# A hybrid decoder step on one core: the samples' float32 products of both output halves in one visit per group, raw weight blocks kept until then, sums in rooms of their own

## The chip, the cores and the metric

One core of a Trainium2 chip runs the whole program; the other seven are idle. The metric is device time in microseconds (us) of that core, the median of three runs. PE is the matrix engine, DVE, ACT and POOL are the vector, scalar and general engines, SP issues most of the DMAs and has one queue, taken in order.

## The reference, cut to what matters

One layer of a hybrid decoder. Its tokens are 256 of a prompt and 64 of samples (8 sequences of 8). The part of interest is the last one, a feed-forward block behind a short convolution over time:

```python
def conv_ffn(h, conv_state, w_up, conv_w, conv_b, w_down):
    up = h @ w_up                                   # 2048 -> 2 x 5632
    up, new_conv = causal_depthwise_conv(up, conv_state, conv_w, conv_b)
    g, u = jnp.split(up, 2, axis=-1)
    return (jax.nn.gelu(g, approximate=True) * u) @ w_down, new_conv   # 5632 -> 2048
```

Its result is normed over the 2048 columns and added to the input. Everything is float32 in and out.

## The kernel before, in words

**Numbers.** A matrix product of the prompt is made of float32r matmuls: a weight block is split into a high part (`whi`, a rounded copy by ACT) and a low part (`wlo`, the rest, by DVE), and three matmuls (hi x hi, hi x lo, lo x hi) make one product. A weight block of 128 x 1024 that is treated so is called a slab. Slabs of the up-projection come through three raw rooms (`wraw`); `whi` and `wlo` have three rooms each too, which slabs and the blocks of the down-projection share in turn. So the copy of a slab can begin only when the matmuls of the third slab or block before it are done.

**Groups.** The 5632 inner columns are taken in 11 groups of 512 (`NG` = 11). `ffn_up(g)` makes group g: 24 matmuls of 128 x 320 for each slab, 16 slabs, then convolution, gelu and product on DVE, ACT and POOL. Between the slabs of `ffn_up(g)` stand the steps of the down-projection of the group before it, `down_steps(g - 1, ...)`, a generator that the loop around the slabs advances. Groups 0 to 9 of the down-projection go through `down_steps`; the last goes through `down_plain`.

**One group of the down-projection.** `down_steps` takes the 2048 output columns in two halves (`m`; group 0 takes half 1 first). A half is a product of 512 x 1024 weights, cut into four raw blocks `b11, b12, b21, b22` of 128 x 1024, loaded by SP. The prompt's part is made with seven products in place of eight (Strassen's scheme in Winograd's form): besides the blocks it takes the differences

- `t1 = b12 - b11`, `t3 = b22 - b12`, `t2 = b22 - t1`, `t4 = t2 - b21`,

which POOL makes in quarters of 256 columns (`less`), in the order given. The seven products come in the order 1 (`b11`), 2 (`b21`), 5 (`t1`), 7 (`t3`), 3 (`b22`), 6 (`t2`), 4 (`t4`), one a step, with a slab between one and the next. Each (`product`) has its block split by ACT and DVE (`ready`) and six matmuls of 128 x 512 (`pm`), and its sum is added by DVE to one of seven kept sums (`taken_in`; in group 0 ACT copies it).

**The samples.** The 64 sample tokens take the blocks as they are, in float32. `sample_products` issues four matmuls for two blocks, on the two column halves of the array; one half's samples are eight matmuls (16 in the trace, which shows each as two), into one PSUM tile `pms`. They stand between products 1 and 2 of each half. So in each group the engine goes twice from float32r to float32 and back. One such stretch of float32 matmuls is called a visit here.

**Rooms.** In a half, `t3` is written over `b12`, `t2` over `b11` and `t4` over `b21`, all after the visit; `t1` has a room of its own. The sums of half 0 lie in the room `in_mix` (where the layer's `acc_mix` was), those of half 1 in `in_fp`. Two rooms under the tag `gain` hold first the four blocks of tokens that are turned in group 0 and stored (`to_rows`, `in_turn`, `x1_rows`), and from group 4 on the last norm's gains, loaded behind that group.

The order of the work on each engine is fixed at build time, by a scheduler that keeps each engine's program in order of priority; `tc.high_priority` and `tc.issue_after` steer it.

Of the kernel before, what the change touches and what calls it, by code (L numbers as in the profile page):

```python
# [16 lines left out]
P = 128  # L17
# [16 lines left out]
def hybrid_step(  # L34
# [111 lines left out]
    bg, side, due, made_so_far, last_made = [], [], {}, [0], [None]  # L146
# [178 lines left out]
    def add_square(total, x, begins, adder=pool, place=("sq", 2)):  # L325
        if begins:
            act.activation(total, x, AF.Square)
        else:
            sq = tp.tile([P, NT], F32, tag=place[0], name="sq", bufs=place[1])
            act.activation(sq, x, AF.Square)  # L330
            adder.tensor_tensor(out=total, in0=total, in1=sq, op=ALU.add)

    def squares_of(total):
# [3 lines left out]
        def step(nb):  # L337
# [6 lines left out]
            with first():  # L344
                if nb < KD - 1:
                    held.append(misc("sq_ps")[:, :NT])
                else:
                    one.append(tp.tile([P, NT], F32, tag="sq", name="sq", bufs=2))
# [80 lines left out]
    with ExitStack() as mctx:  # L429
        op = mctx.enter_context(tc.tile_pool(name="op", bufs=1))  # L430
        bT = op.tile([P, 4, NT], F32, name="bT")
# [157 lines left out]
        with tc.tile_pool(name="gp", bufs=1) as gp:  # L589
# [196 lines left out]
            def gate_mix(g, uf, res):  # L786
# [17 lines left out]
                for m in range(2):  # L804
# [8 lines left out]
                    for i, ps in enumerate(both):  # L813
                        j = 2 * m + i
                        s = tp.tile([P, NT], F32, tag="ev", name="s", bufs=2)
# [44 lines left out]
        with tc.tile_pool(name="sd", bufs=1) as sd:  # L860
# [318 lines left out]
            def heads_out(g):  # L1179
# [4 lines left out]
                def z_evac(j, ps):  # L1184
                    while y_made.get(g, -1) < j:
                        advance(bg, bg[0])
                    zs = tp.tile([P, NT], F32, tag="ev", name="zs", bufs=2)
# [119 lines left out]
    with tc.tile_pool(name="fp", bufs=1) as fp:  # L1307
# [148 lines left out]
        sums_of_m, f_s, taken = [None, None], [None, None], []  # L1456

        def room_for_sums(m):

            room = fp.tile([P, 8, 512], F32, name="in_fp") if m else hp.tile([P, 8, 512], F32, tag="acc_mix", name="in_mix")  # L1460
# [24 lines left out]
        def down_steps(ck, parts):  # L1485
# [8 lines left out]
            last_rows = kept_rows[0]  # L1494
            for _ in range(3 if ck == 0 else 1 if ck == NG - 2 else 2):
                yield
            for m in (1, 0) if ck == 0 else (0, 1):
                raw = {}
                if ck == 0:
                    room_for_sums(m)  # L1500

                def load(name):
                    k, n = int(name[1]) - 1, int(name[2]) - 1
                    raw[name] = fp.tile([P, 1024], F32, name=name)
                    with tc.high_priority(offset=100000), tc.issue_after(slab_load[-1]) if ck == 0 else nullcontext():
                        sp.dma_start(raw[name].rearrange("p (k n) -> p k n", n=512), rows_of(ffn_w_down, 4 * ck + 2 * k, 2, 1024 * m + 512 * n, 512))

                def less(to, x, y):
                    with tc.high_priority(offset=100000), tc.issue_after(last_rows):
                        for q in range(0, 1024, 256):  # L1510
                            cs = slice(q, q + 256)
                            pool.tensor_tensor(out=to[:, cs], in0=raw[x][:, cs], in1=raw[y][:, cs], op=ALU.subtract)  # L1512

                def product(i, x, w):
                    hi, lo = ready(raw[w])
                    ps = misc("pm")
                    prompt_products(ps, (parts.hi[x], parts.lo[x]), (hi, lo), True, True)
                    taken_in(sums_of_m[m][i - 1], ps, ck == 0)

                for name in ("b11", "b12", "b22", "b21"):  # L1520
                    load(name)
                product(1, "a11", "b11")
# [325 lines left out]
```

## Time and profile before

| | |
|---|---|
| three runs | 1740.63 us median (1740.51 to 1740.68) |
| the profiled execution | 1738.82 us, span 1737.1 us, granted PE clock 0.998 |
| PE busy | 1722.9 us, 99% of the span |
| PE's weight loads | 1605.9 us, 92% |
| DVE busy | 1363.9 us, 79% |
| ACT busy | 878.5 us, 51% |
| POOL busy | 684.8 us, 39% |
| DMA | 310.60 MB, 179 GB/s in the mean |

The span is the time from the first to the last instruction; the profiled execution lies 1.72 us above its span, and 1.81 us below the median of the runs. A row of the timeline or of a group names line, engine, operation, what is written and what is read, and shapes as partitions x elements; names come without the numbers of their buffers, so `b11` to `b22` are all `b`, and `t1` is `t`. In square brackets stands idle time of the engine before the instruction and what ended it. Groups 0 to 9 of the down-projection run from about 873 us to 1686 us.

### The profile page before, as it was taken

Reading aid. Unit: us, or ns where it says so; the run is one execution under the profiler, and the core shown is the slowest. Engines: PE = TensorE matmul, PEld = TensorE weight load, DVE = VectorE, ACT = ScalarE, POOL = GpSimd, SP = SyncE. Lnnn points to the kernel's source line nnn. Section 1 sums busy time; section 2 is a strip of 40 time slices with the busy share of each in tenths; the row PEclk is TensorE's granted clock in tenths of the full one; section 3 lists DMA queues with packets and bytes.
Section 4 is the critical chain, followed back from the end, with each engine's and each line's share of the span. In section 5 each row is a group of like instructions: output and inputs, shape, how many; then the busy total and the mean of one; then the engine's idle time right before and its main releaser. Section 6 shows DMA issues by size and latency. Waiting matters only on the chain.

```text
span 1737.1 us, 29944 instructions
## 1 busy us (share of the span) xinstructions
PE 1722.9 (99%) x11223; PEld 1605.9 (92%) x11223; DVE 1363.9 (79%) x2137; ACT 878.5 (51%) x1272; POOL 684.8 (39%) x999
## 2 busy tenths in 40 slices
PE   9999999999999999999999999999999999999997
PEld 9999999999999999999988898888888889888884
DVE  6549864657969788788987778888887879798898
ACT  6344545333656565645565444444444444454443
POOL 2432230000423423112355556565655555555552
PEclk9999999999999999999999999999999999999999
DMA  8786664556676777665765544545445454545445
GB/s 265 215 240 184 185 177 148 157 163 191 202 225 197 227 221 220 205 199 164 241 185 156 158 147 148 159 142 178 150 145 171 144 166 150 164 149 160 148 143 161
DMA packets 216018, 310.60 MB, mean 179 GB/s; under 512 B 22080, under 2 KB 118976, under 8 KB 215680
## 3 DMA queue, kind: packets, MB, share of 16 engines
q1 hardware_dynamic: 198624, 279.76, 53.1%
q0 software_dynamic: 6176, 13.87, 2.6%
q10 hardware_dynamic: 11072, 15.05, 2.5%
q8 instruction: 88, 1.44, 0.4%
q14 instruction: 58, 0.48, 0.1%
HBM read 285.00 MB, written 22.32 MB: 177 GB/s over the span
## 4 chain that ended last, share of the span: by engine, by line
PE 96%; DVE 2%; issue 1%; ACT 0%; POOL 0%; DVEq 0%; ACTq 0%; POOLq 0%
PE ps L135 20%; PE ps L137 20%; PE ps L136 20%; PE pm L1475 11%; PE pd L135 4%; PE pd L137 4%; PE pd L136 4%; PE pms L1482 4%; PE y_ps L1088 1%; PE ps_v L135 1%; PE ps_v L136 1%; PE ps_v L137 1%; DVE wlo L125 0%; PE yo_ps L1003 0%; PE up_ps L1020 0%
## 5 line engine op out<-in xcount | busy, mean ns | idle before, releaser
L135 PE MATMUL ps<-h_hi,whi 128*128 128x320 f32 x2428 | 750.2, 309 | 0.0
L137 PE MATMUL ps<-h_hi,wlo 128*128 128x320 f32 x2428 | 749.0, 309 | 0.1
L136 PE MATMUL ps<-h_lo,whi 128*128 128x320 f32 x2428 | 748.6, 308 | 0.0
L125 DVE TENSOR_TENSOR wlo<-wraw,whi 128x1024 fp32r<-128x1024 f32 (+2 forms) x394 | 487.4, 1238 | 146.0 <-ACT whi L124 144.2
L124 ACT CAST whi<-wraw 128x1024 fp32r<-128x1024 f32 (+2 forms) x393 | 405.1, 1031 | 372.9 <-PE ps L136 143.1
L135 PEld LDWEIGHTS ps<-h_hi,whi 128*128 128x128 f32 x2428 | 455.6, 188 | 9.1 <-issue 1.3
L136 PEld LDWEIGHTS ps<-h_lo,whi 128*128 128x128 f32 x2428 | 455.9, 188 | 6.3
L137 PEld LDWEIGHTS ps<-h_hi,wlo 128*128 128x128 f32 x2428 | 455.5, 188 | 0.7 <-DVE wlo L125 0.6
L1491 DVE TENSOR_TENSOR wlo<-b,whi 128x1024 fp32r<-128x1024 f32 x120 | 155.1, 1292 | 74.4 <-ACT whi L1490 74.2
L1490 ACT CAST whi<-b 128x1024 fp32r<-128x1024 f32 x120 | 125.5, 1046 | 161.9 <-PE ps L136 144.1
L1512 POOL TENSOR_TENSOR b<-b,b 128x256 f32<-128x256 f32 x160 | 184.8, 1179 | 0.0
L135 PE MATMUL pd<-ohi,whi 128*128 128x320 f32 x448 | 138.7, 310 | 0.0
L137 PE MATMUL pd<-ohi,wlo 128*128 128x320 f32 x448 | 138.3, 309 | 0.0
L136 PE MATMUL pd<-olo,whi 128*128 128x320 f32 x448 | 138.3, 309 | 0.0
L1358 POOL COPY ptf<-pad 128x2 f32<-128x2 f32 x88 | 39.2, 446 | 187.2 <-DVE pad L1346 186.6
L1512 POOL TENSOR_TENSOR b<-b,t 128x256 f32<-128x256 f32 x80 | 76.8, 969 | 86.0 <-PE pms L1482 86.0
L1512 POOL TENSOR_TENSOR t<-b,b 128x256 f32<-128x256 f32 x80 | 89.5, 1148 | 14.7 <-DMA b<-in_ffn_w_down 14.7
L135 PEld LDWEIGHTS pd<-ohi,whi 128*128 128x128 f32 x448 | 84.1, 188 | 0.6
L136 PEld LDWEIGHTS pd<-olo,whi 128*128 128x128 f32 x448 | 84.1, 188 | 0.3
L137 PEld LDWEIGHTS pd<-ohi,wlo 128*128 128x128 f32 x448 | 84.1, 188 | 0.0
L248 DVE TENSOR_TENSOR acc_mix<-acc_mix,pd 128x320 f32<-128x320 f32 (+1 forms) x113 | 53.7, 478 | 27.8 <-PE pd L137 27.5
L1482 PE MATMUL pms<-b,a_s 128*64 128x512 f32 x320 | 73.1, 598 | 0.0
(415 smaller groups left out, 2490.4 us busy)
## 6 DMA issues: line engine op xcount, KB each, us to landing
wraw<-in_ffn_w_up SPq DMA_DIRECT2D x176, 512.0 KB, 4.5
wraw<-in_w_in SPq DMA_DIRECT2D x132, 512.0 KB, 3.9
b<-in_ffn_w_down SPq DMA_DIRECT2D x80, 512.0 KB, 4.5
wraw<-in_w_out SPq DMA_DIRECT2D x64, 512.0 KB, 3.5
st<-in_state_ssm SPq DMA_DIRECT2D x40, 256.0 KB, 4.4
out_ssm_state_sample<-st ACTq DMA_DIRECT2D x30, 256.0 KB, 2.4
cs<-dacs_d SPq DMA_DIRECT2D x16, 320.0 KB, 5.3
wraw<-in_w_in SPq DMA_DIRECT2D x12, 384.0 KB, 4.3
```

Of the source, the lines that this page charges most:

```text
L124: rounded[:] = [act.copy(hi, raw).ins]
L125: lowered[:] = [dve.tensor_tensor(out=lo, in0=raw, in1=hi.bitcast(F32), op=ALU.subtract).ins]
L135: pe.matmul(ps, whi, xhi, start=first, stop=False)
L136: pe.matmul(ps, whi, xlo, start=False, stop=False)
L137: last_made[0] = pe.matmul(ps, wlo, xhi, start=False, stop=last).ins
L248: added_last[:] = [dve.tensor_tensor(out=acc[:, nb, ts], in0=acc[:, nb, ts], in1=ps[:, ts], op=ALU.add).ins]
L1358: kept_rows[:] = [pool.tensor_copy(ptf[:, k, :], pad[:, 256:258]).ins]
L1475: last_made[0] = pe.matmul(ps, x[xi][:, k], w[wi][:, 512 * k:512 * k + 512], start=start and k + i == 0, stop=stop and k == 1 and i == 2).ins
L1482: last_made[0] = pe.matmul(ps[64 * h:64 * h + 64], a_s[:, k0 + k], w[h][:, 512 * k:512 * k + 512], start=start and k == 0, stop=stop and k ...
L1490: rounded[:] = [act.copy(hi, raw).ins]
L1491: dve.tensor_tensor(out=lo, in0=raw, in1=hi.bitcast(F32), op=ALU.subtract)
L1512: pool.tensor_tensor(out=to[:, cs], in0=raw[x][:, cs], in1=raw[y][:, cs], op=ALU.subtract)
```

## The change

Three things are changed in `down_steps`, and rooms are moved to fit.

- The samples' products of both halves are made in one place: behind product 1 of the second half, 16 matmuls, into two PSUM tiles. The sums of both are taken in behind them.
- The raw blocks of the first half are therefore kept until then: `t1` and `t2` go to a room `one`, `t3` and `t4` to a room `two`. In the first half `one` has the tag `t1` and `two` the tag `t2`, a new room. In the second half `one` has the tag `t2`, and `two` is the room of that half's own `b11`.
- The blocks of the second half get other rooms than those of the first: `b11` goes to `beside`, two more slices of the room `in_mix`; `b12` and `b22` go to the two rooms under `gain`; `b21` goes to the room under `t1`. Their loads are written at the last two steps of the first half. The last norm's gains are loaded in the last of the ten groups, when the `gain` rooms are free again.

To make place, the mixer's rooms `ev` and `sq` move from the pool `tp`, open all the time, to the pool `op`, which closes behind the mixer. In `down_plain` three rooms for raw blocks are taken in another order. Up to the first group of the down-projection the programs of all engines are otherwise the same.

```diff
-            for m in (1, 0) if ck == 0 else (0, 1):
-                raw = {}
...
+            halves = (1, 0) if ck == 0 else (0, 1)
+            raws = [{}, {}]
...
+            def less(h, to, x, y, room):
+                raw = raws[h]
+                with tc.high_priority(offset=100000), tc.issue_after(last_rows):
+                    for q in range(0, 1024, 256):
+                        cs = slice(q, q + 256)
+                        pool.tensor_tensor(out=room[:, cs], in0=raw[x][:, cs], in1=raw[y][:, cs], op=ALU.subtract)
+                raw[to] = room
...
+            def samples():
+                ps = [misc("pms") for _ in range(2)]
+                for h in range(2):
+                    raw = raws[h]
+                    sample_products(ps[h], parts.a_s, 0, (raw["b11"], raw["b12"]), True, False)
+                    sample_products(ps[h], parts.a_s, 2, (raw["b21"], raw["b22"]), False, True)
+                for h in range(2):
+                    taken_in(f_s[halves[h]], ps[h], ck == 0)
...
-                raw["t1"] = fp.tile([P, 1024], F32, name="t1")
-                less(raw["t1"], "b12", "b11")
-                ps = misc("pms")
-                sample_products(ps, parts.a_s, 0, (raw["b11"], raw["b12"]), True, False)
-                sample_products(ps, parts.a_s, 2, (raw["b21"], raw["b22"]), False, True)
-                taken_in(f_s[m], ps, ck == 0)
-                product(2, "a12", "b21")
+                one = fp.tile([P, 1024], F32, tag="t2" if h else "t1", name="one")
+                less(h, "t1", "b12", "b11", one)
+                if h:
+                    samples()
+                product(h, 2, "a12", "b21")
                 yield
-                raw["t3"] = raw["b12"]
-                less(raw["t3"], "b22", "b12")
-                product(5, "s1", "t1")
+                two = beside[0] if h else fp.tile([P, 1024], F32, tag="t2", name="two")
+                less(h, "t3", "b22", "b12", two)
+                product(h, 5, "s1", "t1")
                 yield
-                raw["t2"] = raw["b11"]
-                less(raw["t2"], "b22", "t1")
-                product(7, "s3", "t3")
+                less(h, "t2", "b22", "t1", one)
+                product(h, 7, "s3", "t3")
...
-                raw["t4"] = raw["b21"]
-                less(raw["t4"], "t2", "b21")
-                product(3, "s4", "b22")
+                less(h, "t4", "t2", "b21", two)
+                product(h, 3, "s4", "b22")
...
+                product(h, 6, "s2", "t2")
+                if h == 0:
+                    if ck == 0:
+                        room_for_sums(halves[1])
+                    load(1, "b11", beside[0])
+                    for name in ("b12", "b22"):
+                        load(1, name, fp.tile([P, SN, 4, 32], F32, tag="gain", name=name, bufs=2).rearrange("p s k f -> p (s k f)")[:, :1024])
                 yield
-                product(4, "a22", "t4")
+                product(h, 4, "a22", "t4")
+                if h == 0:
+                    load(1, "b21", fp.tile([P, 1024], F32, tag="t1", name="b21"))
```

What it does to the programs of the engines is seen at three places. First PE in a group in the middle, where up-projection slabs (`ps`), products (`pm`) and the visit (`pms`) meet in the second half. Before, one tile:

```order
L137 MATMUL ps_7680_3_12952<-h_hi_122,wlo_13047 128x320
L1482 MATMUL pms_13080<-b11_13025,a_s_11688 64x512 [waits DMAHW6_49]
L1482 MATMUL pms_13080<-b12_13027,a_s_11688 64x512 [waits DMAHW2_49]
L1482 MATMUL pms_13080<-b11_13025,a_s_11688 64x512
L1482 MATMUL pms_13080<-b12_13027,a_s_11688 64x512
L1482 MATMUL pms_13080<-b21_13031,a_s_11688 64x512 [waits DMAHW1_49]
L1482 MATMUL pms_13080<-b22_13029,a_s_11688 64x512 [waits DMAHW4_49]
L1482 MATMUL pms_13080<-b21_13031,a_s_11688 64x512
L1482 MATMUL pms_13080<-b22_13029,a_s_11688 64x512
L1475 MATMUL pm_13094<-whi_13090,a12_hi_12509 128x512 [waits Activation_49]
```

After, at the same place, from the end of the first half's tile on:

```order
L1485 MATMUL pms_13070<-b21_12654,a_s_11688 64x512
L1485 MATMUL pms_13070<-b22_12652,a_s_11688 64x512
L1485 MATMUL pms_13071<-in_mix_10381,a_s_11688 64x512 [waits DMAHW5_49,Pool_49]
L1485 MATMUL pms_13071<-b12_12941,a_s_11688 64x512 [waits DMAHW7_49]
L1485 MATMUL pms_13071<-in_mix_10381,a_s_11688 64x512 [waits Pool_49]
L1485 MATMUL pms_13071<-b12_12941,a_s_11688 64x512
L1485 MATMUL pms_13071<-b21_12991,a_s_11688 64x512 [waits DMAHW7_49]
L1485 MATMUL pms_13071<-b22_12943,a_s_11688 64x512 [waits DMAHW2_49]
L1485 MATMUL pms_13071<-b21_12991,a_s_11688 64x512
L1485 MATMUL pms_13071<-b22_12943,a_s_11688 64x512
L1478 MATMUL pm_13094<-whi_13090,a12_hi_12509 128x512 [waits Activation_49]
```

The eight matmuls that stood in the first half now stand ahead of the second half's eight, and the first half goes from product 1 through a slab to product 2. Groups 1 to 9 are all like this.

Second, group 0. There PE's program after has the second tile in two pieces, with product 2 and nine matmuls of the next slab between them:

```order
L1485 MATMUL pms_10509<-b12_10383,a_s_9653 64x512
L1485 MATMUL pms_10509<-b21_10429,a_s_9653 64x512 [waits DMAHW5_49]
L1478 MATMUL pm_10532<-whi_10528,a12_hi_9913 128x512 [waits Activation_49]
```

```order
L137 MATMUL ps_6144_1_10336<-h_hi_122,wlo_10542 128x320
L1485 MATMUL pms_10509<-b22_10385,a_s_9653 64x512 [waits DMAHW1_49]
L1485 MATMUL pms_10509<-b21_10429,a_s_9653 64x512
L1485 MATMUL pms_10509<-b22_10385,a_s_9653 64x512
L135 MATMUL ps_6144_1_10336<-h_hi_122,whi_10541 128x320
```

and SP's queue has the load that they wait for, `b22_10385`, behind the last store of turned tokens and behind two loads for group 1 (`b11_10920`, `b12_10922`), which wait for the visit itself to have read the blocks in their rooms:

```order
L1321 DMA x1_rows_114<-in_turn_10329 32x10x128 [waits DMAHW4_49]
L118 DMA wraw_10713<-in_ffn_w_up 128x4x256 [waits DMAHW6_49,DMAHW5_49,DVE_49]
L1321 DMA x1_rows_114<-in_turn_10329 32x10x128
L1505 DMA b11_10920<-in_ffn_w_down 128x2x512 [waits DMAHW7_49,PE_49]
L1505 DMA b12_10922<-in_ffn_w_down 128x2x512 [waits DMAHW0_49,PE_49]
L1505 DMA b22_10385<-in_ffn_w_down 128x2x512 [waits DMAHW4_49,DMAHW6_49,DMAHW2_49,DMAHW1_49]
L1505 DMA b22_10924<-in_ffn_w_down 128x2x512 [waits PE_49]
```

Before, the same stretch of SP's queue had all blocks of the second half ahead of it, and these rows:

```order
L1506 DMA b21_10469<-in_ffn_w_down 128x2x512 [waits DMAHW2_49,DVE_49]
L118 DMA wraw_10586<-in_ffn_w_up 128x2x512 [waits DMAHW3_49,DVE_49]
L1320 DMA x1_rows_114<-in_turn_10338 32x10x128 [waits DMAHW4_49]
L1320 DMA x1_rows_114<-in_turn_10338 32x10x128 [waits DMAHW5_49]
L118 DMA wraw_10632<-in_ffn_w_up 128x4x256 [waits DMAHW6_49,DVE_49]
```

So in group 0 there are two visits after, as before, the first of 13 matmuls and the second of three.

Third, POOL in the second half of the last of the ten groups. Before, `t2` (in `b11`) and `t3` (in `b12`) are made in turns of a quarter, both behind the visit (`PE`):

```order
L1512 TENSOR_TENSOR b11_18187<-b22_18191,t1_18237 128x256 [waits DMAHW3_49,PE_49,Activation_49]
L1512 TENSOR_TENSOR b12_18189<-b22_18191,b12_18189 128x256 [waits PE_49]
L1512 TENSOR_TENSOR b12_18189<-b22_18191,b12_18189 128x256
L1512 TENSOR_TENSOR b11_18187<-b22_18191,t1_18237 128x256
L1512 TENSOR_TENSOR b11_18187<-b22_18191,t1_18237 128x256 [waits PE_49]
```

After, `t2` (`one`) comes first and waits for DVE's split of `t1`, and `t3` (`in_mix`, the room of `b11`) follows:

```order
L1513 TENSOR_TENSOR one_18223<-b22_18074,one_18223 128x256 [waits DMAHW0_49,DVE_49]
L1513 TENSOR_TENSOR one_18223<-b22_18074,one_18223 128x256 x3
L1513 TENSOR_TENSOR in_mix_10381<-b22_18074,b12_18072 128x256 [waits PE_49]
L1513 TENSOR_TENSOR in_mix_10381<-b22_18074,b12_18072 128x256
L1513 TENSOR_TENSOR in_mix_10381<-b22_18074,b12_18072 128x256 [waits PE_49]
```

Groups 1 to 8 have the same order after. The wait of `t2` is no longer for the visit; that of `t3` is for its matmuls that read `b11`.

More of the change, by code (lines that the diff above doesn't have):

```diff
@@ L328, in add_square @@
         else:
-            sq = tp.tile([P, NT], F32, tag=place[0], name="sq", bufs=place[1])
+            sq = mixer[0].tile([P, NT], F32, tag=place[0], name="sq", bufs=place[1])
             act.activation(sq, x, AF.Square)
@@ new lines, in down_steps @@
+            if ck == 0:
+                room_for_sums(halves[0])
+            for name in ("b11", "b12", "b22", "b21"):
+                load(0, name, fp.tile([P, 1024], F32, name=name))
+            for h in range(2):
+                raw = raws[h]
+                product(h, 1, "a11", "b11")
+                yield
+                one = fp.tile([P, 1024], F32, tag="t2" if h else "t1", name="one")
[3 more added lines that the diff above has]
+                product(h, 2, "a12", "b21")
@@ L1652, in hybrid_step @@
         pool.memset(squares, 0.0)
-        gain = []
         for g in range(1, NG):
@@ L1660, in hybrid_step @@
                 advance(bg, steps)
-            if g == 4:
-                with tc.issue_after(slab_load[-1]):
-                    for m in range(2):
-                        gain.append(fp.tile([P, SN, 4, 32], F32, tag="gain", name="gain", bufs=2).rearrange("p s k f -> p (s k f)"))
-                        sp.dma_start(gain[m][:, :1024], norm_last[0:1, 1024 * m:1024 * m + 1024].broadcast_to([P, 1024]))
         held_w = hp.tile([P, 4, 1024], F32R, tag="h_hi", name="held_w")
```

63 lines of the change are left out of this document (31 added, 32 removed).

## The prediction

> **What bounds the kernel now.** I read the page first, then the chain, then what PE waits for, then the visits one by one. The page and the chain:
>
> ```profile
> PE 1722.9 (99%) x11223; PEld 1605.9 (92%) x11223; DVE 1363.9 (79%) x2137; ACT 878.5 (51%) x1272; POOL 684.8 (39%) x999
> PE 96%; DVE 2%; issue 1%; ACT 0%; POOL 0%; DVEq 0%; ACTq 0%; POOLq 0%
> ```
>
> PE is busy almost all the time, and 96% of the chain that ended last is PE's. So the time is PE's program plus the few places where PE waits. The list of waits has for PE only three:
>
> ```profile
> PE early L69 <- DVE ones L65: 1.1, 1, 1.1
> PE pm L1475 <- DVE wlo L1491: 1.1, 1, 1.1
> PE pd L1475 <- DVE a_lo L399: 0.7, 1, 0.7
> ```
>
> In the ten groups there is one wait, of 1.1 us. Loads, copies and POOL are hidden today. The change can therefore gain in PE's own program, or by removing that wait, and it can lose by making PE wait where it does not yet.
>
> The visits, as the rows of the tile `pms` have them, and one visit in PE's timeline, with PE's weight loads below and a place without a visit (a slab followed by a product) last:
>
> ```profile
> L1482 PE MATMUL pms<-b,a_s x320: 592/592/644, 878.1 to 1662.3; 128*64 128x512 f32 x160
> ...
>   POOL b L1512: 86.0, 20
> ```
>
> ```profile
> 957.68 0.31 PE L136 MATMUL ps<-h_lo,whi 128*128 128x320 f32 x1
> 957.82 0.31 PE L137 MATMUL ps<-h_hi,wlo 128*128 128x320 f32 x1
> 958.06 3.65 PE L1482 MATMUL pms<-b,a_s 128*64 128x512 f32 x16
> 961.64 0.50 PE L1475 MATMUL pm<-whi,a_hi 128*128 128x512 f32 x1
> 961.98 0.40 PE L1475 MATMUL pm<-whi,a_lo 128*128 128x512 f32 x1
> ...
> 1667.70 0.31 PE L137 MATMUL ps<-h_hi,wlo 128*128 128x320 f32 x1
> 1667.85 0.39 PE L1475 MATMUL pm<-whi,s_hi 128*128 128x512 f32 x1
> 1668.08 0.39 PE L1475 MATMUL pm<-whi,s_lo 128*128 128x512 f32 x1
> ```
>
> ```profile
> 958.54 0.14 PEld L1482 LDWEIGHTS pms<-b,a_s 128*64 128x64 f32 x2 [0.29 <-issue]
> ...
> 960.69 0.14 PEld L1482 LDWEIGHTS pms<-b,a_s 128*64 128x64 f32 x2 [0.29 <-issue]
> ```
>
> From the last slab matmul to the second `pm` it takes 961.98 - 957.82 = 4.16 us with a visit and 1668.08 - 1667.70 = 0.38 us without, so a visit costs 3.78 us. The weight loads come in pairs, one for each half of the array, with six from 958.54 to 960.69: a step is 2.15 / 5 = 0.43 us. Sixteen matmuls are eight steps, 3.44 us. The remaining 0.34 us is paid at the edges: 0.24 for 0.15 before the first pair, a first step of 0.48, a late first `pm`, and 0.34 for 0.23 behind it. All 20 visits have this shape (durations 592/592/644).
>
> **The change part by part.**
>
> *Visits.* The matmuls stay the same in number, so the steps stay. Before there are 20 visits. After there are one in each of nine groups and two in group 0, 11 in all. Nine fewer at 0.34 us: -3.1 us, all on PE, so all on the path. Two sum tiles in one visit are not in the trace. From below, the second tile costs nothing; from above, it costs the whole edge again, and the term is 0. I take nothing, since of the edge's parts only the first step's 0.05 us lies inside the visit.
>
> *Group 0, the visit in two pieces.* Cutting the tile behind its fifth product leaves a matmul alone on its half of the array in each piece: at most two products (two steps each in pairs) of 0.86 us that ran beside another. From 0 (they overlap neighbours) to +0.9; I take +0.6.
>
> *Group 0, the late block.* The last piece waits for `b22`. Call V the start of the visit. SP issues the load after the last store of turned tokens has landed. That store stands behind a slab's load, which before the change went out just ahead of the second visit:
>
> ```profile
> 914.95 0.39 SPq L118 DMA_DIRECT2D wraw<-in_ffn_w_up  x1
> 915.38 0.51 SPq L1320 DMA_DIRECT2D x_rows<-in_turn  x1
> ...
> wraw<-in_ffn_w_up SPq DMA_DIRECT2D x1, 512.0 KB, 3.8
> x_rows<-in_turn SPq DMA_DIRECT2D x1, 160.0 KB, 3.8
> 916.32 3.58 PE pms L1482 x16
> ```
>
> So the store goes out at V - 0.9 and lands at V + 2.9. In between SP issues two loads for group 1, as soon as four products (four steps, 1.7 us) have read their rooms. All 16 stores and all 80 loads landed within these bounds:
>
> ```profile
> DMA to landing us min/median/max: 2.3/4.2/5.8
> DMA to landing us min/median/max: 3.7/4.5/9.5
> ```
>
> With the load's median, `b22` is there at V + 7.4, and with 5.5, which such a load took right behind another one (below), at V + 8.4. PE reaches the last piece after 13 products in 14 steps (6.0 us), product 2 (six at 0.23, 1.4) and nine slab matmuls at 0.15 (1.3): V + 8.9 with the edges. So it is hidden, barely. From 0 to +3 us (a store of 5.8 and a load behind two others); I take +0.3. What hangs on `b22` behind that: POOL's `t3` (four quarters, 3.7 us at the median of 910 ns), its two splits (2.3), needed five stretches later (1.7 + 2.2 + 1.4 + 3.5 = 8.8 us). That holds.
>
> *The first half's blocks are kept.* The loads of the next group's first half now wait for the visit's end and stand on SP ahead of slabs. They cost nothing as long as a slab behind them could not have gone anyway: its room is freed by the split of the slab three before, which waits for PE. The slab behind the five loads is freed by a split that follows product 2, so some 3 us behind the visit, and PE needs it four slabs and five products later (21 us). Loads at 4.5 us leave more than 10 us. SP then waits for POOL's `t3` and DVE's split of `b22` before two further loads, at about V + 11 and V + 19, and each time the next slab's room comes free as late. Cover: the three `wraw` rooms and the pace of PE. Nothing.
>
> *POOL.* The second half's `t2` no longer waits for the visit but for the split of `t1`, `t3` follows. Before, in a middle group:
>
> ```profile
> 1497.23 1.23 DVE L1491 TENSOR_TENSOR wlo<-t,whi 128x1024 fp32r<-128x1024 f32 x1 [1.82 <-ACT whi L1490]
> 1497.43 1.62 POOL L1512 TENSOR_TENSOR b<-b,t 128x256 f32<-128x256 f32 x1 [3.69 <-PE pms L1482]
> ...
> 1504.16 0.73 POOL L1512 TENSOR_TENSOR b<-b,t 128x256 f32<-128x256 f32 x1
> ```
>
> Eight quarters take 7.5 us (1497.43 to 1504.16 + 0.73) and wait 3.69 us for the visit to read the blocks in their rooms. After, they begin when the split ends, V + 2.4, and end at V + 10; product 7 needs `t3` split (2.3 us) at V + 16.7, since the visit is 3.4 us longer. Slack grows by 2 us. `one` and `two` in the first half wait for no visit at all. Nothing, and the 86.0 us of POOL's waits shrink without effect.
>
> *The last group's wait.* Here the rows of four engines:
>
> ```profile
> 1678.06 0.39 PE L1475 MATMUL pm<-whi,s_lo 128*128 128x512 f32 x1
> 1679.57 0.50 PE L1475 MATMUL pm<-wlo,s_hi 128*128 128x512 f32 x1 [1.12 <-DVE wlo L1491]
> 1680.75 0.31 PE L136 MATMUL ps<-h_lo,whi 128*128 128x320 f32 x1
> 1681.18 0.41 PE L137 MATMUL ps<-h_hi,wlo 128*128 128x320 f32 x1
> 1660.45 2.71 POOL L1512 TENSOR_TENSOR b<-b,t 128x256 f32<-128x256 f32 x1 [2.97 <-PE pms L1482]
> 1670.26 1.05 ACT L1490 CAST whi<-b 128x1024 fp32r<-128x1024 f32 x1 [4.88 <-POOL b L1512]
> 1671.35 1.37 DVE L1491 TENSOR_TENSOR wlo<-b,whi 128x1024 fp32r<-128x1024 f32 x1 [2.41 <-ACT whi L1490]
> 1678.30 1.22 DVE L1491 TENSOR_TENSOR wlo<-b,whi 128x1024 fp32r<-128x1024 f32 x1
> ```
>
> POOL makes `t3` late, ACT sits 4.88 us, DVE 2.41 us, and DVE's queue is then late with the split of `b22` by 1.5 us and of the next slab by 0.3: 1.51 - 0.23, 0.34 - 0.23 and 0.43 - 0.15 make 1.7 us of PE. Counted from product 2, `t3` comes some 2 us earlier after the change (above), and DVE gets 1.4 us. I take -1.4, ends 0 and -1.7. What is late next is DVE's queue itself: a split for `down_plain` (1.2 us) moves ahead of it, into DVE's idle 2.4 us.
>
> *The rest.* `ev` and `sq` in another pool change no program ahead of the groups. In `down_plain` some DVE work changes places; -0.5 to +0.7, taken as +0.1.
>
> *Sum.* -3.1 + 0.6 + 0.3 - 1.4 + 0.1 = -3.5 us. The profiled execution took 1738.82 us, so it would take 1735.3; it lies 1.8 below the median, 1740.63, which gives 1737.1. I say **1737.2**. About 0.2%, 3.5 us, is what a measurement here can tell from no change (1737.15 and 1744.1), so the forecast lies at that line.
>
> **The rivals.**
>
> *The edge goes with the tile, not the visit.* Then -3.1 is 0, the sum -0.4, 1740.2. For it: no row has two tiles in one visit. Against: only 0.05 of the 0.34 us lies inside. By the Trainium skill, page TensorEngine Tiling, Key Properties, a change of tiling mode drains the engine and a change of tile does not; by that the edge goes with the visit, which speaks against this rival; the trace agrees in that each visit pays both ways.
>
> *Block `b22` is late in group 0.* Loads on one queue share the engines. Two 512 KB loads issued 0.5 us apart before:
>
> ```profile
> 891.05 0.40 SPq L118 DMA_DIRECT2D wraw<-in_ffn_w_up  x1
> 891.55 0.91 SPq L1506 DMA_DIRECT2D b<-in_ffn_w_down  x1
> ...
> wraw<-in_ffn_w_up SPq DMA_DIRECT2D x1, 512.0 KB, 3.8
> b<-in_ffn_w_down SPq DMA_DIRECT2D x1, 512.0 KB, 5.5
> ```
>
> They landed at 894.8 and 897.0, 2.2 us apart. If all queued loads go in strict order, the two for group 1 land at V + 5.6 and 7.8 and `b22` at V + 10.0: a wait of 1.1 us in place of 0.3, and 1738.0. The Trainium skill, page DMA: Bandwidth & Descriptors, section Queues, rings and completion order, says that each DMA engine takes one queue's descriptors in ring order; by it this rival holds.
>
> *The last group's wait stays.* DVE's queue may be late for its own work. Then 1738.6.
>
> *Slower: slabs late behind the kept blocks.* Place: SP, where five loads wait for the visit and then for POOL's `t3`, with slabs behind. If a slab came late by x in nine groups, PE would lose 9x; it decides from (3.5 + 3.5) / 9 = 0.8 us on. With 1.5 us it gives 1750.6. Against it stand the 10 us of slack.
>
> *The clock.* Through a visit it was at 1.00 in this row of a stretch of time (busy times of PE, its weight loads, DVE, ACT and POOL, then the granted clock, the share of DMA and GB/s):
>
> ```profile
> 958.00:961.70 3.70, 3.70 (x18) 1.12 (x17) 2.51 (x3) 1.04 (x1) 2.33 (x2) 1.00 0.38 117
> ```
>
> A visit of 7.2 us could be taken for idleness; at half speed for one visit's length (3.65 us) behind it PE loses 1.8 us nine times, 1753.6. The Trainium skill, page TensorE: Matmul & The Clock Gate, Part 1, puts the window in which activity is judged at about 3.4 us, so that a visit now fills one for the first time twice over; no run here shows a clock that fell in a visit.
>
> **How the numbers follow.** Forecast 0.57, its own spread 1735.6 to 1738.6, so a little more than half of it beyond the line: 0.30 faster, 0.27 same. Edge by tile 0.07, late `b22` 0.13, wait stays 0.10: all same. A tail of `down_plain` that gains 1 us more, 1736.2: 0.05, faster. Slabs late 0.06, clock 0.02: slower. That makes 0.35, 0.57 and 0.08. The range from 1735.2 to 1741.8 leaves out the slower cases and a little at both ends.
>
> **What would show it.** One `pms` group of 32 a group from group 1 on, 7.1 us long; two in group 0, with a PE wait under 1 us for a DMA of `b`; no wait of `pm` for DVE near the end of the last group; SP's slabs as early before their use as now. I am wrong if PE's list of waits has rows of several us, or if the edges inside a visit of two tiles show a gap.

## The result: 39 us slower, and where the profile after shows it

The changed kernel takes 1779.35 us (median of six runs, 1778.43 to 1781.38) beside 1740.57 us for the kernel before: a ratio of 1.0224, with a 95% interval of 1.0213 to 1.0235. The prediction said 1737.2 us. The profiled execution took 1781.38 us with a span of 1779.7 us, 42.6 us more than the span before; it is the slowest of the six, and the ledger below divides its 42.6 us. The page after, first busy times, then the chain that ended last, by engine:

```profile
PE 1735.9 (98%) x11223; PEld 1610.5 (90%) x11223; DVE 1351.6 (76%) x2137; ACT 876.2 (49%) x1272; POOL 636.8 (36%) x999
PE 84%; DVE 7%; POOL 5%; issue 2%; ACT 1%; DMA 1%; ACTq 0%; SPq 0%; DVEq 0%; POOLq 0%
```

PE's share of the chain fell from 96% to 84%, and POOL, which had 0%, has 5%. PE's list of waits (us in total, times, longest) names what PE waits for:

```profile
PE pm L1478 <- DVE a_lo L399: 15.9, 14, 1.5
PE ps L137 <- DVE wlo L125: 9.7, 11, 1.5
PE ps L135 <- ACT whi L124: 3.5, 8, 1.5
PE both_halves L1749 <- DVE most L1720: 1.8, 1, 1.8
...
PE pms L1485 <- DMA b<-in_ffn_w_down: 1.0, 1, 1.0
```

Before, three waits made 2.9 us. Now PE waits about 31 us for DVE and ACT, and almost nothing for DMA. In groups 1 to 9 nearly all of these waits come at one place, between the first half's product 1 and its product 5. There the convolution of one group of `ffn_up` ends and the next group begins. PE's rows in the timeline at the start of group 5, those with a wait:

```profile
1308.27 0.50 PE L1478 MATMUL pm<-whi,a_lo 128*128 128x512 f32 x1 [0.79 <-DVE a_lo L399]
1310.00 0.42 PE L135 MATMUL ps<-h_hi,whi 128*128 128x320 f32 x1 [0.30 <-ACT whi L124]
1311.37 0.41 PE L137 MATMUL ps<-h_hi,wlo 128*128 128x320 f32 x1 [0.81 <-DVE wlo L125]
1316.58 0.50 PE L1478 MATMUL pm<-whi,a_lo 128*128 128x512 f32 x1 [1.48 <-DVE a_lo L399]
```

The visit itself is as forecast. The rows around it in the same group, from the last slab matmul to the second `pm`:

```profile
1350.66 0.31 PE L137 MATMUL ps<-h_hi,wlo 128*128 128x320 f32 x1
...
1357.92 0.50 PE L1478 MATMUL pm<-whi,a_hi 128*128 128x512 f32 x1
1358.25 0.39 PE L1478 MATMUL pm<-whi,a_lo 128*128 128x512 f32 x1
```

That is 7.59 us, less 0.38 without a visit: 7.21 us for two tiles beside 2 x 3.78 us before. So a merged visit saves 0.35 us, the edge.

**A ledger by products.** Product starts (the first `pm` of each) can be set beside each other, since PE's program is the same. Where no visit lies between two products and nothing waits, they stand 4.91 us apart. With the old visit between products 1 and 2 it was 8.58 us, and 5.03 from 2 to 5 (the late first `pm`). At the start of group 5, the first `pm` of products 1 and 2, and of product 5 before (after, it starts 6.67 us behind product 2):

```profile
1286.35 0.39 PE L1475 MATMUL pm<-whi,a_hi 128*128 128x512 f32 x1
1294.92 0.50 PE L1475 MATMUL pm<-whi,a_hi 128*128 128x512 f32 x1
1299.95 0.39 PE L1475 MATMUL pm<-whi,s_hi 128*128 128x512 f32 x1
```

```profile
1307.03 0.46 PE L1478 MATMUL pm<-whi,a_hi 128*128 128x512 f32 x1
1314.71 0.40 PE L1478 MATMUL pm<-whi,a_hi 128*128 128x512 f32 x1
```

| | product 1 | to product 2 | to product 5 | late at product 2, at product 5 |
|---|---|---|---|---|
| before | 1286.35 | 8.58 | 5.03 | 0, 0 |
| after | 1307.03 | 7.68 | 6.67 | 2.77, 1.76 |

Late means beyond the distance without a wait: 4.91 us, or with a visit as before. So 4.53 us are lost in this group. The idle times of the four rows above make 3.38 of them; the rest lies in the matmuls on either side of each stop. Groups 2 to 8 are alike within 0.03 us, and groups 1 and 9 lose 4.2 each. Of the 42.6 us, 40.0 are these nine places, 4.4 lie in group 0 and 1.8 behind the last product; nine merged visits give back 3.2, and the last group's second half 0.4. The experiments divide the 4.53 us.

### The profile page after: what moved, and what is told of

The parts are those of the page before. It is cut to its first block, busy times and chain, and to the rows that moved or that the text cites. A ratio compares the mean times of both kernels' runs of the same rounds, so it can differ in the third digit from the quotient of the medians.

```text
span 1779.7 us, 29877 instructions
## 1 busy us (share of the span) xinstructions
PE 1735.9 (98%) x11223; PEld 1610.5 (90%) x11223; DVE 1351.6 (76%) x2137; ACT 876.2 (49%) x1272; POOL 636.8 (36%) x999
## 4 chain that ended last, share of the span: by engine, by line
PE 84%; DVE 7%; POOL 5%; issue 2%; ACT 1%; DMA 1%; ACTq 0%; SPq 0%; DVEq 0%; POOLq 0%
PE ps L137 17%; PE ps L135 17%; PE ps L136 17%; PE pm L1478 8%; PE pd L135 4%; PE pd L137 4%; PE pd L136 4%; PE pms L1485 4%; POOL one L1513 2%; POOL two L1513 1%; DVE wlo L1494 1%; DVE wlo L125 1%; DVE ucv L1356 1%; ACT whi L1493 1%; DMA raw<-in_ffn_w_down 1%
## 5 line engine op out<-in xcount | busy, mean ns | idle before, releaser
L1513 POOL TENSOR_TENSOR one<-b,one 128x256 f32<-128x256 f32 x80 | 70.0, 905 | 116.9 <-DVE wlo L1494 116.9
L1494 DVE TENSOR_TENSOR wlo<-b,whi 128x1024 fp32r<-128x1024 f32 x50 | 68.0, 1361 | 30.9 <-ACT whi L1493 30.7
L1493 ACT CAST whi<-b 128x1024 fp32r<-128x1024 f32 x50 | 52.3, 1045 | 64.9 <-PE ps L136 59.2
L1356 DVE SCALAR_TENSOR_TENSOR ucv<-pad,prm,ucv 128x336 f32<-128x336 f32 x88 | 57.4, 662 | 24.9 <-ACT ucv L1354 24.2
L1494 DVE TENSOR_TENSOR wlo<-one,whi 128x1024 fp32r<-128x1024 f32 x40 | 48.8, 1220 | 32.5 <-ACT whi L1493 32.1
```

The lines of the kernel that those rows point to most:

```text
L1356: dve.scalar_tensor_tensor(out=t[:, :n], in0=pad[:, r:r + n], scalar=col(prm_at[f"fw{r}"][0] + k), in1=t[:, :n], op0=ALU.mult, op1=ALU.add)
L1493: rounded[:] = [act.copy(hi, raw).ins]
L1494: dve.tensor_tensor(out=lo, in0=raw, in1=hi.bitcast(F32), op=ALU.subtract)
L1513: pool.tensor_tensor(out=room[:, cs], in0=raw[x][:, cs], in1=raw[y][:, cs], op=ALU.subtract)
```

## The experiments

Four theories were set against each other. Theory 1: POOL's `t3`, which no longer waits for a visit, now stands ahead of a small copy in POOL's queue, and a chain of queues hands the delay on. Theory 2: POOL's early differences and DVE slow each other. Theory 3: kept blocks make loads late. Theory 4, formed after the first experiments: the old visit had been the cover for DVE's work. The rows that suggested theory 1, POOL and ACT in the timeline, before and after:

```profile
1275.49 4.84 POOL L1512 TENSOR_TENSOR t<-b,b 128x256 f32<-128x256 f32 x4
1280.28 0.47 POOL L1357 COPY stg<-pad 128x16 f32<-128x16 f32 x1
...
1280.78 0.34 ACTq L1405 DMA_DIRECT2D out_ffn_conv_sample<-stg  x1
1281.17 0.67 ACT L1353 ACTIVATE ucv<-pad,prm 128x336 f32<-128x336 f32 x1 [4.36 <-POOL stg L1357]
```

```profile
1296.18 4.84 POOL L1513 TENSOR_TENSOR one<-b,b 128x256 f32<-128x256 f32 x4
1300.98 3.35 POOL L1513 TENSOR_TENSOR two<-b,b 128x256 f32<-128x256 f32 x4
1304.27 0.20 POOL L1358 COPY stg<-pad 128x16 f32<-128x16 f32 x1
...
1304.49 0.34 ACTq L1406 DMA_DIRECT2D out_ffn_conv_sample<-stg  x1
1304.88 0.67 ACT L1354 ACTIVATE ucv<-pad,prm 128x336 f32<-128x336 f32 x1 [7.39 <-POOL stg L1358]
1305.46 1.03 ACT L1493 CAST whi<-b 128x1024 fp32r<-128x1024 f32 x1
```

ACT issues the store of `stg`, so it waits for POOL's copy: 4.36 us before, 7.39 us after, because `t3` (`two`) went in between. Behind that DMA in ACT's queue stand the convolution and the split for product 1 (`whi<-b`).

**1. The copy ahead of the differences.**

```
-                pool.tensor_copy(stg[:, half, j], tokp[:, :, 8:10])
-                kept_rows[:] = [pool.tensor_copy(ptf[:, k, :], pad[:, 256:258]).ins]
+                pool.tensor_copy(ptf[:, k, :], pad[:, 256:258])
+                kept_rows[:] = [pool.tensor_copy(stg[:, half, j], tokp[:, :, 8:10]).ins]
```

> The changed kernel, with one swap: of POOL's two copies behind each convolution the one into stg is written second, and the differences t1 to t4 may be issued only behind it. So stg is done ahead of t1 and t3 in POOL's queue; all other work, t3's early place included, stays. Theory 1 (a queue): in the changed kernel t3 stands in POOL's queue ahead of the last copy into stg, ACT's DMA of stg waits for that copy, and ACT's splits and then DVE's stand behind the DMA. It expects the 4.2 to 4.5 us lost between two groups to go in nine groups, and 2.2 us in group 0: 42 us, so about 1741 us. Theory 2 (shared work): POOL's two differences run now while DVE is busiest and each slows the other. They still do here: about 1779 us, as the changed kernel. Theory 3 (loads): the kept blocks hold up SP's queue and slabs come late: about 1779 us too.

Measured: 1764.13 us, 1.0131 [1.0116, 1.0146]. Theory 1 holds for 1.81 us of a group's 4.53 (the distance from product 1 to 2 goes from 7.68 to 5.87 us), not for all. ACT's wait is gone from its list, yet PE still waits at two places:

```profile
1302.41 0.41 PE L137 MATMUL ps<-h_hi,wlo 128*128 128x320 f32 x1 [0.69 <-DVE wlo L125]
...
1307.62 0.50 PE L1478 MATMUL pm<-whi,a_lo 128*128 128x512 f32 x1 [1.47 <-DVE a_lo L399]
```

**2. The DMA taken from ACT.**

```
-                act.dma_start(o_fconv_s[:, k:k + 4], stg[:, half])
+                pool.dma_start(o_fconv_s[:, k:k + 4], stg[:, half])
```

> The changed kernel with its POOL order untouched; only the DMA that stores stg is issued by POOL in place of ACT. Theory 1 in its exact form (ACT's queue is the link between POOL and the splits) expects 1741 us, give or take 2 for the cost of issuing on POOL, and no long wait of ACT for stg. If the link is instead DVE's own wait for rooms that POOL fills behind t3, the loss stays: about 1779 us. Theories 2 and 3: 1779 us.

Measured: 1762.78 us, 1.0125 [1.0110, 1.0140], the same as the first (5.80 and 6.66 us between the products). POOL's order is untouched here, so the link that handed POOL's delay on is ACT's queue alone.

**3. Half of the delay.**

```
...
-                with tc.high_priority(offset=100000), tc.issue_after(last_rows):
-                    for q in range(0, 1024, 256):
+                for q in range(0, 1024, 256):
+                    with tc.high_priority(offset=100000), tc.issue_after(last_stg if to == "t3" and h == 0 and q >= 512 else last_rows):
```

`last_stg` is the group's last copy into `stg`.

> The changed kernel with t3 of the first half cut: two of its quarters stay ahead of the last copy into stg, two may go only behind it. The copy is then late by half of what it was (about 1.7 of 3.4 us). Theory 1, if the loss grows in proportion: half of 42 us, about 1759 us. Theory 1 with slack in the chain: some 0.6 us (DVE's wait at that place before the change) are free, then the loss follows the delay: (1.7 - 0.6) of (3.4 - 0.6), 17 us, about 1756 us. Theories 2 and 3: 1779 us.

Measured: 1766.18 us, 1.0143 [1.0126, 1.0160]. Both figures of theory 1 had given the queue all 42 us; beside the 1764 us of experiment 1, which removes the whole delay, half a delay costs only 2 us. The distance from product 1 to 2 is 6.29 us: the first two quarters ahead of the copy cost 0.42 us a group, the other two 1.39. The first part of the delay falls into slack; what comes behind it reaches PE.

**4. The early `t3` alone, in the kernel before.**

```
...
-                raw["t3"] = raw["b12"]
+                raw["t3"] = fp.tile([P, 1024], F32, tag="t2", name="two") if m == (ck == 0) else raw["b12"]
```

In the lines left out, `ev` and `sq` move to the pool `op` as in the change.

> The kernel before, two visits a group, with one part of the change: t3 of the first half is written into a room of its own (the mixer's two rooms ev and sq move to make place) and so need not wait for the visit. The visits, loads and kept blocks are as before. POOL's queue then has t1, t3, stg in this order, as after the change. Theory 1 expects the loss of the changed kernel in all ten groups without any visit merged: 40 to 42 us, about 1781 us. Theory 3 (loads behind kept blocks) expects no loss: 1741 us. Theory 2 expects a loss as theory 1.

Measured: 1772.78 us, 1.0181 [1.0166, 1.0196]. Without a merged visit, product 2 comes 11.38 us behind product 1, 2.80 more than before; that is the 2.77 of the changed kernel at this place. No block is kept here, so these 2.8 us are not theory 3's. The distance to product 5 (5.01) has no wait where the changed kernel has 1.76 us; some 0.5 us come one product later.

The rows that suggested theory 4 were there before the change. Busy times of a stretch of the kernel before (its length, then PE, PE's weight loads, DVE, ACT, POOL), first from product 4, the last of a group, to product 5 of the next group, then from product 1 to product 3 of the second half, where the merged visit went:

```profile
1274.40:1299.95 25.55, 25.55 (x156) 22.03 (x155) 24.75 (x39) 11.98 (x17) 16.50 (x22) 1.00 0.41 125
...
1324.48:1348.00 23.52, 23.52 (x139) 19.75 (x138) 14.41 (x15) 8.78 (x10) 13.33 (x14) 1.00 0.44 127
```

DVE's 79% is a mean. In the first stretch it is 97% busy (24.75 of 25.55), and 3.8 us of the stretch are the visit, PE work that needs no split. In the second DVE has 61%. The change took the visit from where DVE needs it and put it where it does not. In the kernel of experiment 1 the same stretch is DVE's, 24.27 of 24.46 us:

```profile
1287.94:1312.40 24.46, 22.30 (x140) 20.95 (x139) 24.27 (x39) 11.89 (x17) 13.84 (x20) 1.00 0.41 131
```

**5. Visits apart again, all else as in experiment 1.**

```
...
-                if h:
-                    samples()
+                samples(h)
```

`samples(h)` makes the products of one half into one tile.

> The changed kernel with stg copied second (as in the first experiment) and the samples' visits apart again, one tile in each half as before the change; rooms, loads and POOL's order stay as in the first experiment, and the first half's t1 and t3 are still made early, beside DVE. Theory 4 (cover): the visit of the first half, 3.8 us of PE that need no work of DVE, stood in the stretch in which DVE is 97% busy; without it PE's program there is shorter than DVE's, and PE waits for the splits behind product 1. It expects PE's 2.7 us of waits a group to go and nine visits to cost 0.35 us each again: about 1743 us, no PE wait over 1 us at product 2. Theory 2 (POOL's early differences slow DVE) expects the waits to stay: 1764 + 3 = 1767 us.

Measured: 1758.99 us, 1.0108 [1.0094, 1.0122]. The wait at product 2 is gone (5.02 us to product 5) with the blocks kept as before, as theory 4 says and theory 3 does not. The other stays: 9.54 us to product 2 in group 5, 0.96 more than before, and 0.95 to 1.04 more in groups 2 to 8. So experiment 1's 0.96 is not the visit's, and theory 4's 1743 us are missed by 16. The profiled span is 19.0 us above the one before: 6.8 us are these seven groups, 7.8 lie in group 0 (up to group 1's product 2) and 4.1 in the last group, behind product 5 of its second half.

**6. `t3` out of the full stretch, merged visit kept.**

```
-                with tc.high_priority(offset=100000), tc.issue_after(last_rows):
+                with tc.high_priority(offset=100000), tc.issue_after(rounded[0] if to == "t3" and h == 0 else last_rows):
```

> The first experiment (merged visit in the second half, stg copied second) with t3 of the first half ordered behind the split for product 2; in POOL's program it then stands ahead of the convolution's copies and of t1, outside of the stretch in which DVE is full. With the visits apart 0.96 us a group were left that a visit doesn't explain; if they are POOL's t3 beside DVE, the loss in each group goes from 2.7 to about 1.7 us (the missing cover alone): 1764 - 9 = 1755 us. If t3 beside DVE costs nothing, it stays at 1764 us. If t3 waits there for its blocks and holds up the convolution's copies, it is slower than 1764 us, with ACT waiting for POOL.

Measured: 1751.74 us, 1.0063 [1.0051, 1.0076]. The counterpart of experiment 5: product 2 comes 4.91 us behind product 1, no wait, and 6.43 us lie between 2 and 5. PE's one wait there:

```profile
1302.10 0.50 PE L1478 MATMUL pm<-whi,a_lo 128*128 128x512 f32 x1 [1.25 <-DVE a_lo L399]
```

DVE's rows show what moving `t3` saves it. First the same stretch as shown for experiment 1, then three steps of the convolution on DVE, in experiment 1 and here:

```profile
1283.61:1306.89 23.28, 22.03 (x140) 20.93 (x139) 22.13 (x39) 11.99 (x17) 11.70 (x16) 1.00 0.45 138
...
1292.67 2.98 DVE L1356 SCALAR_TENSOR_TENSOR ucv<-pad,prm,ucv 128x336 f32<-128x336 f32 x3
...
1290.16 1.64 DVE L1356 SCALAR_TENSOR_TENSOR ucv<-pad,prm,ucv 128x336 f32<-128x336 f32 x3
```

The same 39 instructions of DVE take 22.13 us in place of 24.27. That is theory 2: it holds for this part of the loss, and 0.96 of the 2.14 us reach PE.

The two waits come apart cleanly (us that the product is late, in group 5):

| | at product 2 | at product 5 |
|---|---|---|
| after | 2.77 | 1.76 |
| 1: copy first | 0.96 | 1.73 |
| 5: copy first, visits apart | 0.96 | 0 |
| 6: copy first, `t3` elsewhere | 0 | 1.52 |

So a group's 4.53 us are 1.81 us for POOL's queue and ACT's DMA, 0.96 us for `t3` beside DVE, and 1.76 us for the missing cover.

**7. DVE loaded in the kernel before.**

```
-                        combined("s1", "a21", ALU.add, "a22")
+                        for _ in range(7):
+                            combined("s1", "a21", ALU.add, "a22")
```

> The kernel before the change, with one sum of the token blocks (s1 = a21 + a22, 128x256) written seven times in place of once: six more DVE instructions a group at the end of the convolution, nothing else. At 0.34 to 0.42 us they are 2.0 to 2.5 us. Theory 4: DVE had 0.8 us of idle time in that stretch (25.15 of 25.95 us busy), so 1.2 to 1.7 us a group reach PE: 12 to 17 us over ten groups, 1753 to 1758 us. If DVE's share there is no limit (79% over the span, loss from POOL or from loads): within 1 us of the kernel before.

Measured: 1777.88 us, 1.0216 [1.0202, 1.0230]. That DVE has no room there is confirmed, but the size is missed: 4.7 us between products 5 and 7 of group 5 in place of 1.2 to 1.7. DVE's and ACT's rows show why:

```profile
1306.43 0.88 DVE L1436 TENSOR_TENSOR s<-a 128x256 f32<-128x256 f32 x2
...
1311.30 2.70 DVE L1436 TENSOR_TENSOR s<-a 128x256 f32<-128x256 f32 x3
...
1317.47 0.41 ACT L398 CAST s_hi<-s 128x256 fp32r<-128x256 f32 x1 [7.39 <-DVE s L1436]
1318.66 1.04 ACT L124 CAST whi<-wraw 128x1024 fp32r<-128x1024 f32 x1
```

The sums take 0.44 us each while POOL rests and 0.90 us while it makes differences, and ACT waits 7.39 us for a sum with a slab's copy behind it.

**8. The other terms of the ledger, on top of experiment 1.**

```
-                        load(1, name, fp.tile([P, SN, 4, 32], F32, tag="gain", name=name, bufs=2).rearrange("p s k f -> p (s k f)")[:, :1024])
+                        load(1, name, fp.tile([P, 1024], F32, name=name) if ck == 0 else fp.tile([P, SN, 4, 32], F32, tag="gain", name=name, bufs=2).rearrange("p s k f -> p (s k f)")[:, :1024])
...
-                        raw = None if 3 <= n < 6 else fp.tile([P, 1024], F32, tag=("b22", "b21", "t1")[n % 6], name="raw")
+                        raw = None if 3 <= n < 6 else fp.tile([P, 1024], F32, tag=("t1", "b22", "b21")[n % 6], name="raw")
```

In group 0 each half also makes its samples alone.

> The first experiment (stg copied second), with the two other losses undone: group 0 keeps its two visits and loads b12 and b22 of the second half into the rooms of the first half's, and the last group's raw rooms are taken in the old order. By the rows of the first experiment group 0 lost 5.2 us, of which about 1.9 lie at its second visit, and the stretch behind the last group some 2 us. Expected: 1764 - 4, about 1760 us; no wait of PE for b22, group 0's second visit in one piece. By theory 4 the 2.7 us a group at the first half's products stay.

Measured: 1761.21 us, 1.0123 [1.0109, 1.0136], 2.9 below experiment 1 in another set of runs. Group 0's wait for `b22` is gone. The order of the raw rooms is not what costs the time behind the last product: 1.4 of the 1.8 us stay.

**9. The visit merged on the other side.** If cover is what counts, the second half's samples should be carried into the next group's first visit.

```
+                mine = dict(raw), parts.a_s, halves[h], ck == 0
+                if h == 0:
+                    samples([mine] + carried)
+                    carried.clear()
+                elif ck == NG - 2:
+                    samples([mine])
+                else:
+                    carried.append(mine)
```

The second half's blocks lie in `beside`, the two `gain` rooms and the room `t2`; in the first half `t3`, `t2` and `t4` go over its own blocks.

> The merged visit put where the cover is needed: the products of the second half's samples are carried into the next group and made in one visit with that group's first half, between its products 1 and 2. The second half's four raw blocks are kept for it in rooms of their own; the first half's differences go over its own blocks behind the visit, as before the change. Only the last of the ten groups makes its second half's samples alone: 11 visits in place of 20. Theory 4: DVE's full stretch gets 3.4 us more cover, the stretch left without a visit has DVE at 61%, so no wait comes; nine edges of 0.35 us are saved: 1741 - 3.1, about 1738 us. Theory 2 or 3: no reason for a gain; loads of kept blocks make it slower by several us.

Measured: 1749.79 us, 1.0054 [1.0041, 1.0068]. From group 2 to group 7 there is no wait and each group is 0.36 us shorter, as expected. What makes it slower is above all one wait in group 0, here PE's row and POOL's:

```profile
935.39 0.80 PE L1478 MATMUL pm<-whi,s_hi 128*128 128x512 f32 x1 [8.87 <-ACT whi L1493]
...
931.50 2.76 POOL L1513 TENSOR_TENSOR two<-b,b 128x256 f32<-128x256 f32 x4 [12.09 <-DMA b<-in_ffn_w_down]
```

ACT waits there for `t3` (`two`), and `t3` for `b22`, whose room still held turned tokens: the prediction's late block, at another product.

**10. The same, with group 0 and the last group as before the change.**

```
+            kept = ck not in (0, NG - 2)
...
-                    carried.append(mine)
+                elif not kept:
+                    samples([mine])
+                else:
+                    carried.append(mine)
```

Where nothing is kept, the second half's blocks go to the rooms of the first half's.

> The carried visit (second half's samples made with the next group's first half), mended where its trace showed the loss: 12.3 us in group 0, where PE waited 8.9 us for a split of t3, which waited for b22, whose load stood behind the stores of turned tokens. Group 0 and the last group now keep nothing: their second halves load into the rooms of the first and make their samples alone, as before the change (the last group's t3 and t4 still have a room of their own). 12 visits in place of 20. Expected: eight edges at 0.36 us, the step that the carried visit showed in each group from 2 on, make 2.9 us; the last group gains up to 1.4 us as there; no PE wait over 1.2 us: 1740.5 - 2.9 - 1.4 = 1736 us, and 1738 if the last group gives nothing. If DVE's full stretch is not what decides, there is no reason for less than the 1750 us of the carried visit.

Measured: 1735.49 us beside 1740.19, 0.997 [0.9958, 0.9981]: faster than both kernels, with 12 visits in place of 20. PE's whole list of waits, and its busy times from product 4 of one group to product 5 of the next:

```profile
PE early L69 <- DVE ones L65: 1.1, 1, 1.1
PE both_halves L1758 <- DVE most L1729: 0.5, 1, 0.5
PE pd L1478 <- DVE a_lo L399: 0.2, 1, 0.2
```

```profile
1270.34:1299.31 28.97, 28.97 (x173) 23.18 (x171) 27.17 (x41) 11.98 (x17) 19.92 (x26) 1.00 0.54 170
```

DVE has 27.17 us of work in a stretch that now lasts 28.97: 1.8 us to spare where it had 0.8.

## Why the prediction was wrong, by its own steps

- **The bound (failed).** "Loads, copies and POOL are hidden today" was read from means and from PE's short list of waits. That PE waited nowhere at a group's start did not say by how much: DVE had 0.8 us of 25.55 left. The part on the visits counted what a visit costs PE and never asked what it covers. No rival had it; the list of rivals looked at the edges, loads, the clock and the end. This step lost 1.76 us a group.
- **POOL (failed).** "`one` and `two` in the first half wait for no visit at all. Nothing" took a wait's end for a gain. An instruction that no longer waits moves up in its queue; what stood behind its wait now stands behind its work, here `stg`, ACT's DMA and ACT's splits (1.81 us a group), and it ran beside DVE at its fullest (0.96 us). The order of POOL's program in the second half was read; the one in the first half, which holds these 2.77 us, was not.
- **The edges (right).** -0.34 us a visit was forecast; 0.35 to 0.36 were measured in every merged visit. The edge goes with the visit, not the tile. The Trainium skill, page TensorEngine Tiling, section Key Properties, says that a change of tiling mode drains the engine; the rows change from 128*128 to 128*64 and back only at the two ends of a visit, however many sums it makes, and the trace agrees.
- **Group 0 (right in kind, short in size).** The piece behind `b22` waited 1.0 us, not 0.3: the rival that put all queued loads in strict order had said 1.1. The rows below show PE's second piece. The whole second half lost 1.9 us against the old one, 0.9 forecast. The first half lost 2.2 us too, forecast at nothing: 1.5 up to product 2, which experiment 4 loses as well, where only `t3` has another room, and 0.7 up to product 5, which are gone with the visits apart in experiment 5.

```profile
925.19 1.93 PE L1485 MATMUL pms<-b,a_s 128*64 128x512 f32 x6 [0.96 <-DMA b<-in_ffn_w_down]
```

- **The last group (smaller).** -1.4 us forecast, -0.4 measured: the old wait went (-1.5), but product 7 came 1.06 us later, behind a slab whose split by DVE was late (PE idle for 0.78 us). In experiment 10 the term reached -1.6.
- **Behind the last product (missed).** +0.1 forecast, +1.8 measured. PE waits there for DVE (`both_halves` for `most`, 1.8 us in the list above). In experiment 10, where the last norm's gains are loaded earlier, 0.3 us are left, but in experiment 6, which loads them as the changed kernel does, no more than 0.6. So those loads alone are not the cause, and it stays open.
- **Slabs behind the kept blocks, and the clock (right).** PE has no wait for a slab's load, and the granted clock stays at 1.00 through a visit twice as long:

```profile
1350.66:1357.90 7.24, 7.24 (x35) 2.25 (x33) 1.91 (x2) 1.04 (x1) 4.58 (x7) 1.00 0.76 222
```

## What to carry to other kernels

Before work is moved from one stage to another, read each engine's busy share in both stages, not over the span: an engine that shows 79% in the mean can be at 97% in the stage that loses its cover, and the stretch of PE work that looks like pure cost may be what hides it. When a wait is taken away, follow the freed instructions to their new place in the queue and ask who now stands behind them, DMA issues on a compute engine's queue above all. Where merging is worth having, merge to the side that is short of cover.

## What the runs showed of the hardware

- POOL and DVE slow each other, instruction by instruction. A 128x256 difference on POOL takes 0.73 us alone and up to 1.77 us at a group's start; a 128x256 sum on DVE 0.44 and 0.90 us (experiment 7). POOL's row, nanoseconds min/median/max:

```profile
L1513 POOL TENSOR_TENSOR one<-b,b x40: 727/1003/1772, 865.8 to 1649.5; 128x256 f32<-128x256 f32 x40
```

  The Trainium skill, page SBUF — State Buffer, section SBUF: two separate sides, says that the two share one pair of ports and that the first to start holds it for its whole instruction, also where DVE reads two operands of SBUF. The rows agree. A split on DVE that began 0.06 us ahead of a difference kept its 1.23 us, and the difference took 1.78 (experiment 1, at 1289.1 us); a split that began 0.08 us behind one took 1.74 us, and the difference 0.73 (the changed kernel, at 1296.2 us). So the rule spoke against this change; what it cost is the 0.96 us a group.
- PE's clock fell in a long wait. Behind the 8.87 us of experiment 9 the granted clock was 0.50 and six matmuls took 0.63 to 0.80 us in place of 0.40:

```profile
926.00:935.39 9.39, 0.52 (x4) 0.26 (x2) 0.02 (x1) 1.10 (x2) 3.89 (x6) 0.76 0.31 91
935.39:938.60 3.21, 3.06 (x6) 1.99 (x7) 3.21 (x3) 2.00 (x3) 3.21 (x3) 0.50 0.01 3
```
